# Second blocks of tokens of a pair's two heads share a step of differential attention; the second layer's memory logits two blocks at a time

## The chip, the cores and the metric

The kernel runs on one core of a Trainium2 chip. A core has a matrix engine (TensorE, PE in the profile, with its weight loads as PEld), a vector engine (VectorE, DVE), a scalar engine (ScalarE, ACT), a general engine (GpSimd, POOL) and an engine that issues most transfers (SyncE, SP). Each runs its own list of instructions in order and waits on semaphores for the others. The metric is device time in microseconds (us) for one execution, the median of several runs; lower is better.

## The reference, cut to what matters

Two layers on 512 tokens of width 1024. Layer 0 mixes tokens by differential attention: 6 heads, each with two query/key maps of width 64 and values of width 128. Tokens are handled in 4 blocks of 128 rows; block i of a head sees keys up to its own chunk, so it needs 128(i+1) keys. Layer 1 mixes by gated linear attention (4 heads). In both layers a cross attention of 4 heads into 256 memory tokens runs beside it, and both results go through one output projection; a gated MLP follows.

```python
logits = jnp.einsum('bhmqd,bhmkd->bhmqk', qb, k)         # m: the two maps of a head
logits = jnp.where(visible, logits + bias, -jnp.inf)
p = jax.nn.softmax(logits, axis=-1)
w = p[:, :, 0] - lam * p[:, :, 1]
o = jnp.einsum('bhqk,bhkv->bhqv', w, v)
...
o = rms_norm(o, out_norm_g) * (1.0 - lam_init)
# beside it, in both layers:
p = jax.nn.softmax(jnp.einsum('bqhd,bkhd->bhqk', q, k), axis=-1)   # k, v: 256 memory tokens
cross = jnp.einsum('bhqk,bkhd->bqhd', p, v)
x = x + jnp.concatenate([mix, cross], axis=-1) @ w_out[i]
```

## The kernel before

**Order.** The order of TensorE's instructions is the program's own, written out by hand. ACT, DVE, POOL and SP get their order from a scheduler at compile time, which takes what is ready by its reckoning, earlier written instructions first; once compiled, each of these lists is fixed too.

**Filler.** The large products are cut into units and put into a queue `F` (class `Filler`). `gemm` makes units of 6 matmuls of 512 columns, 1.296 us of credit each; `out_proj` units of 3 matmuls, 0.65 us. `F.fill(us)` adds credit and emits units until it is used up; `F.need(name)` emits until a marked point; `F.flush()` emits all. Every product is three matmuls (high and low parts of the split operands; ACT makes the high part of a weight block at L203, DVE the low part at L206).

**The loop of layer 0** (`diff_layer`) has 18 steps, three for a head: blocks 2 and 0 together (512 columns), block 1 alone (256 columns), block 3 alone (512). A turn t of the loop writes, for TensorE: `logits(t)` (L648, both maps, into the two PSUM banks with tag `lg`), `values(t-2)` (L686, into a bank `sm` that a head keeps until its last block), every third turn `finish` of an earlier head, filler, `turn(t-1)` (transposes of the finished weights, bank `tp`, copied out by ACT at L674), the memory attention's part, and filler again. There are two banks of each tag (`lg`, `sm`, `tp`, `mm`), used in rotation: whoever takes a bank waits until its last reader is done.

Beside TensorE a step goes: DVE adds the bias and takes the maximum (L653), ACT takes the exponential (L656), DVE inverts sums and joins the two maps (L661, L662, L664). When a head's last block has its values, ACT squares (L692), both normalise, and DVE writes `o` (L696). `finish(h)` transposes `o` into a bank `tp`, and ACT (L260) and DVE (L261) read the bank into the split tiles `mix[h]` that the output projection takes.

`prepare(h)` transposes queries and keys of a head into two `tp` banks, ACT copies both (`qT`, `kT`, L615); `logits` of that head need both. `norms(pair)` normalises queries and keys of a pair on ACT and DVE (L333, L334, L337). `keys1` makes the second layer's memory keys in a bank `lg` (ACT at L506). `MemAttn.logits(b)` writes one block of tokens into the two banks `lg` (L537); DVE and ACT do its softmax (L540, L544, L548); `MemAttn.turn(u)` transposes half a block (bank `tp`, copied at L557 by DVE or ACT); `MemAttn.values(pair)` takes a bank `sm` (L571) and splits it by L260 and L261, twice in turn.

**Layer 1** (`gla_layer`): four gate products (L858) into banks `lg` and `sm` in turn, read by DVE at L863 and L865, then the memory attention in a loop of 6 turns with `F.fill(4.0)` each, then the heads, `gate(1)`, `F.fill(8.0)` and `finish(1)`, which transposes three tiles with `F.fill(1.2)` after each, and a flush. Its transposes need `rr`, written by DVE at L980.

Of the kernel before, what the change touches and what calls it, by code (L numbers as in the profile page):

```python
# [11 lines left out]
F32 = mybir.dt.float32  # L12
# [9 lines left out]
S = 512  # L22
# [11 lines left out]
STEPS, FILL = (11, 18), (3.7, 1.64, 1.5)  # L34

TOGETHER = ((2, 0), (1,), (3,))
# [95 lines left out]
def trunk(ctx, tc, head_d, x_t, mem_t, wpack, cols_a_d, cols_d, conv_d, gate_d, rel_bias, diff_lambda, consts, onehot, out):  # L132
# [381 lines left out]
    class MemAttn:  # L514
# [16 lines left out]
        def logits(self, b):  # L531
            sm, rc = small("smm")[:, :4], small("rcm")[:, :4]
            pl = bank("lg"), bank("lg")
            for hp in range(2):
                for j in range(2):
                    hh = blk(j, 64)
                    mm(pl[j][:, blk(hp, 256)], self.qT[hp][hh, blk(b)], kmT[self.l][hh, hp], start=True, stop=True)  # L537
# [23 lines left out]
        def values(self, pair):  # L561
# [3 lines left out]
            po = bank("sm")  # L565
# [12 lines left out]
    def diff_layer(pool, mix, acc):  # L578
# [22 lines left out]
        heads = {}  # L601
# [5 lines left out]
        def prepare(h):  # L607
            pr, j = divmod(h, 2)
            t2 = []
            for src, g, nm in zip(qk[pr], (c_dq, c_dk), ("qT", "kT")):  # L610
                dst = pool.tile([128, S], F32, name=nm, bufs=3)
                p = bank("tp")
                for b in range(NB):
# [3 lines left out]
            sm = cp.tile([128, 16], F32, name="smd", tag="smd")  # L617
            heads[h] = dict(q=t2[0], k=t2[1], s2=sm.rearrange("p (m b) -> p m b", b=8),
                            nm=small("nmd"), rc=small("rcd"), v=vs[pr], j=j)
# [4 lines left out]
        def members(t):  # L624
            h, s = divmod(t, 3)
            out, at = [], 0
            for i in TOGETHER[s]:
                out.append((i, slice(at, at + 128 * (i + 1)), at))
                at += 128 * (i + 1)
            return h, out, at  # L630

        def logits(t):
            h, group, _ = members(t)
            H = heads[h]
            s2, nm, rc = H["s2"], H["nm"], H["rc"]
            if t % 3 == 0:
                bt = H["bt"] = pool.tile([128, S], F32, name="bt", bufs=2)
                src = bass.AP(tensor=bias_d.tensor, offset=bias_d[h].offset + 1, ap=[[1, 128], [1, 512]])
                nc.sync.dma_start(bt, src)
                G.memset(bt[0:64, 0:64], -1e30)  # L640
            pls = bank("lg"), bank("lg")
            for i, _, at in group:
                nk = 128 * (i + 1)
                cuts = (0, nk) if i == 0 else (0, nk // 2, nk)
                for k0, k1 in zip(cuts, cuts[1:]):
                    for m in range(2):
                        hh = blk(m, 64)
                        mm(pls[m][:, at + k0:at + k1], H["q"][hh, blk(i)], H["k"][hh, k0:k1], start=True, stop=True)  # L648
            e = xtile(), xtile()
            for m in range(2):  # L650
                for i, c, _ in group:
                    n1 = nm[:, 2 * i + m:2 * i + m + 1]
                    V.tensor_tensor_reduce(  # L653
                        out=e[m][:, c], in0=pls[m][:, c], in1=H["bt"][:, 127 + 128 * i::-1], scale=-1.0,
                        scalar=1e38, op0=ALU.add, op1=ALU.min, accum_out=n1)
                    A.activation(e[m][:, c], e[m][:, c], AF.Exp, scale=-1.0, bias=n1,  # L656
                                 accum_out=s2[:, m, i:i + 1])
            ids = sorted(i for i, _, _ in group)
            b = slice(ids[0], ids[-1] + 1, 2)
            lr = rc[:, 4 + ids[0]:4 + ids[-1] + 1:2]  # L660
            V.reciprocal(rc[:, b], s2[:, 1, b])  # L661
            V.scalar_tensor_tensor(lr, rc[:, b], nlam, s2[:, 0, b], op0=ALU.mult, op1=ALU.mult)  # L662
            for i, c, _ in group:
                V.scalar_tensor_tensor(e[1][:, c], e[1][:, c], rc[:, 4 + i:5 + i], e[0][:, c],  # L664
                                       op0=ALU.mult, op1=ALU.add)
# [11 lines left out]
        def values(t):  # L677
            h, group, _ = members(t)
            H = heads[h]
            if t % 3 == 0:  # L680
                F.need(f"v{h // 2}")
                H["po"] = bank("sm")
            po, wT = H["po"], live.pop(t)
            for i, _, at in group:
                for kb in range(i + 1):
                    mm(po[:, blk(i)], wT[:, at + 128 * kb:at + 128 * kb + 128], H["v"][:, kb, blk(H["j"])],  # L686
                       start=kb == 0, stop=kb == i)
            if t % 3 == 2:
                rs, ss, sq = small("rs0")[:, :NB], small("ss")[:, :NB], xtile()
# [537 lines left out]
```

## Time and profile before

| | |
|---|---|
| median of 3 runs | 1180.74 us (1180.72 to 1180.92) |
| the profiled execution | 1180.98 us |
| its span (first to last instruction) | 1179.2 us |
| what lies around the span | 1.78 us |
| TensorE busy | 1168.3 us of the span |
| VectorE, ScalarE busy | 757.1 us, 547.1 us |
| granted TensorE clock, mean | 0.999 |

Layer 0's loop stands at about 44 to 232 us of the span, layer 1's memory attention at 641 to 676 us, its `finish(1)` at 793 to 798 us. A matmul's shown duration overlaps the next one's, so the pace of TensorE is read from start to start, and its idle time from the view of waits. A row of the waits reads: engine, bank and line that waited, what ended the wait, total us, times, longest us.

### The profile page before, as it was taken

What the parts mean: (1) busy time and instruction counts of PE and PEld (TensorE: products, weight loads), DVE (VectorE), ACT (ScalarE), POOL (GpSimd) and SP (SyncE); (2) the same over time, 40 slices, a digit from 0 to 9 for tenths busy, and PEclk for the clock granted to TensorE, in tenths of its full rate; (3) what the DMA queues carried; (4) which work ended last, traced back from release to release, by engine and by line L of the source; (5) the groups of instructions that cost most, each with busy time, mean ns of one, the idle gap of its engine ahead of it and who ended that gap; (6) DMA issues with size and microseconds to landing.
All of it is one profiled execution on the core that took longest, in us unless ns stands there. A gap on an engine that the chain in (4) does not pass through costs nothing.

```text
span 1179.2 us, 14803 instructions
## 1 busy us (share of the span) xinstructions
PE 1168.3 (99%) x5658; PEld 966.6 (82%) x5658; DVE 757.1 (64%) x1252; ACT 547.1 (46%) x952; POOL 4.6 (0%) x25
## 2 busy tenths in 40 slices
PE   9999999999999999999999999999999999999998
PEld 7887877888888888888887888987888888888887
DVE  7567677597767335777557656768776743476741
ACT  6676576565444213344437534536443422343420
POOL 0000000000000000000000000000000000000000
PEclk9999999999999999999999999999999999999999
DMA  8432214132323232223341221243232233232231
GB/s 287 140 94 95 76 51 138 59 125 99 116 72 108 89 108 92 104 73 108 126 144 56 72 72 58 76 151 109 72 122 92 81 116 107 72 125 73 80 108 44
DMA packets 39556, 117.68 MB, mean 100 GB/s; under 512 B 4703, under 2 KB 7192, under 8 KB 39486
## 3 DMA queue, kind: packets, MB, share of 16 engines
q1 hardware_dynamic: 39054, 116.35, 29.3%
q8 instruction: 44, 0.72, 0.3%
q10 hardware_dynamic: 432, 0.39, 0.1%
q14 instruction: 26, 0.21, 0.1%
HBM read 112.52 MB, written 4.21 MB: 99 GB/s over the span
## 4 chain that ended last, share of the span: by engine, by line
PE 95%; ACT 2%; DVE 2%; issue 1%; POOL 0%; DVEq 0%; ACTq 0%; POOLq 0%
PE ps_mm L299 9%; PE ps_mm L298 9%; PE ps_mm L300 9%; PE ps_sm L300 7%; PE ps_sm L299 7%; PE ps_sm L298 7%; PE ps_mm L279 5%; PE ps_mm L281 5%; PE ps_mm L280 5%; PE ps_lg L298 3%; PE ps_lg L299 3%; PE ps_lg L300 3%; PE ps_tp L298 3%; PE ps_tp L299 3%; PE ps_tp L300 3%; PE ps_tp L172 2%
## 5 line engine op out<-in xcount | busy, mean ns | idle before, releaser
L203 ACT CAST whi<-raw 128x1024 fp32r<-128x1024 f32 (+4 forms) x212 | 207.7, 985 | 244.5 <-PE ps_tp L299 120.9
L206 DVE TENSOR_TENSOR wlo<-raw,whi 128x1024 fp32r<-128x1024 f32 (+4 forms) x212 | 240.6, 1140 | 94.0 <-ACT whi L203 91.4
L298 PE MATMUL ps_mm<-xsh,whi 128*128 128x512 f32 x438 | 173.0, 395 | 0.0
L299 PE MATMUL ps_mm<-xsl,whi 128*128 128x512 f32 x438 | 170.6, 390 | 0.8 <-DVE xsl L261 0.8
L300 PE MATMUL ps_mm<-xsh,wlo 128*128 128x512 f32 x438 | 170.6, 390 | 0.0
L298 PE MATMUL ps_sm<-xsh,whi 128*128 128x512 f32 x378 | 147.1, 389 | 0.0
L300 PE MATMUL ps_sm<-xsh,wlo 128*128 128x512 f32 x378 | 147.1, 389 | 0.0
L299 PE MATMUL ps_sm<-xsl,whi 128*128 128x512 f32 x378 | 147.0, 389 | 0.0
L279 PE MATMUL ps_mm<-whi,xsh 128*128 128x512 f32 (+2 forms) x352 | 136.1, 387 | 0.1
L281 PE MATMUL ps_mm<-whi,xsl 128*128 128x512 f32 (+2 forms) x352 | 131.0, 372 | 0.4 <-DVE xsl L261 0.4
L280 PE MATMUL ps_mm<-wlo,xsh 128*128 128x512 f32 (+2 forms) x352 | 130.6, 371 | 0.0
L1084 ACT ACTIVATE cvo<-u,cv 128x512 f32<-128x512 f32 x88 | 71.6, 815 | 123.1 <-DVE u L1082 123.1
L299 PEld LDWEIGHTS ps_mm<-xsl,whi 128*128 128x128 f32 x438 | 82.3, 188 | 18.1 <-DVE xsl L261 1.1
L298 PEld LDWEIGHTS ps_mm<-xsh,whi 128*128 128x128 f32 x438 | 82.3, 188 | 17.3 <-issue 0.5
L300 PEld LDWEIGHTS ps_mm<-xsh,wlo 128*128 128x128 f32 x438 | 82.2, 188 | 17.2
L1085 DVE SCALAR_TENSOR_TENSOR cvo<-u,cv,cvo 128x512 f32<-128x512 f32 x88 | 65.9, 750 | 39.8 <-ACT cvo L1084 39.7
L300 PEld LDWEIGHTS ps_sm<-xsh,wlo 128*128 128x128 f32 x378 | 71.0, 188 | 14.7
L298 PEld LDWEIGHTS ps_sm<-xsh,whi 128*128 128x128 f32 x378 | 71.0, 188 | 14.7
L299 PEld LDWEIGHTS ps_sm<-xsl,whi 128*128 128x128 f32 x378 | 71.0, 188 | 14.7
L279 PEld LDWEIGHTS ps_mm<-whi,xsh 128*128 128x128 f32 x352 | 66.2, 188 | 13.6 <-issue 3.3
L281 PEld LDWEIGHTS ps_mm<-whi,xsl 128*128 128x128 f32 x352 | 66.1, 188 | 12.4 <-DVE xsl L261 0.6
L280 PEld LDWEIGHTS ps_mm<-wlo,xsh 128*128 128x128 f32 x352 | 66.4, 189 | 9.9
(273 smaller groups left out, 1745.6 us busy)
## 6 DMA issues: line engine op xcount, KB each, us to landing
raw<-in_wpack_dram SPq DMA_DIRECT2D x178, 512.0 KB, 3.5
xt<-in_x_t_dram SPq DMA_DIRECT2D x15, 256.0 KB, 4.8
raw<-in_wpack_dram SPq DMA_DIRECT2D x15, 256.0 KB, 3.0
raw<-in_wpack_dram SPq DMA_DIRECT2D x8, 384.0 KB, 3.9
xres<-xt SPq DMA_DIRECT2D x8, 256.0 KB, 2.3
xt<-xres SPq DMA_DIRECT2D x8, 256.0 KB, 4.2
out_dram<-xt SPq DMA_DIRECT2D x7, 256.0 KB, 2.0
bt<-bias_d SPq DMA_DIRECT2D x6, 256.0 KB, 4.6
```

Source lines behind the costliest of these rows:

```text
L172: nc.tensor.transpose(dst, src, ident[:n, :n])
L203: ins = A.copy(hi[:, c], raw[:, c])
L206: V.tensor_sub(lo[:, c], raw[:, c], hi[:, c].bitcast(F32))
L279: mm(p, sh[k][:, blk(b)], hi, start=k == 0, stop=False)
L280: mm(p, sh[k][:, blk(b)], lo, start=False, stop=False)
L281: mm(p, sl[k][:, blk(b)], hi, start=False, stop=k == KT - 1)
L298: mm(p, hi[:, blk(n)], bh, start=i == first, stop=False)
L299: mm(p, hi[:, blk(n)], bl, start=False, stop=False)
L300: mm(p, lo[:, blk(n)], bh, start=False, stop=i == last)
L1084: A.activation(c, u[:, 2:], AF.Identity, scale=cv[l][:, 2, j:j + 1], bias=cv[l][:, 3, j:j + 1])
L1085: V.scalar_tensor_tensor(c, u[:, 1:S + 1], cv[l][:, 1, j:j + 1], c, op0=ALU.mult, op1=ALU.add)
```

## The change

Layer 0's attention is grouped by pairs of heads, 5 steps of 512 columns for a pair: blocks 2 and 0 of the first head, its block 3, block 1 of both heads, blocks 2 and 0 of the second head, its block 3. So 15 steps take the place of 18, in a loop of 18 turns in place of 21. The matmuls of each block stay as they are.

With it go: new filler credits (`STEPS`, `FILL`), the second share of a turn cut in two halves, with `prepare` between them (before: at the turn's end); `prepare` of a pair's first head one turn ahead of its first logits, and in the turns after a `prepare` the logits stand behind `values`; `norms`, `finish`, `load_x`, `out_proj`, `keys1` in other turns; layer 0's memory values in a bank `lg` in place of `sm`, and its memory logits in turns 5, 6, 7 and 9. In layer 1 the memory logits take two blocks at a time, the second block in the two banks `sm`; the loop's filler is (5.0, 4.0, 3.5, 5.0, 4.0, 2.5) in place of 6 times 4.0, and the fill ahead of `finish(1)` is 5.6 in place of 8.0.

```diff
-STEPS, FILL = (11, 18), (3.7, 1.64, 1.5)
-TOGETHER = ((2, 0), (1,), (3,))
+STEPS, FILL = (8, 11), (4.75, 2.1, 1.55)
+TOGETHER = (((0, 2), (0, 0)), ((0, 3),), ((0, 1), (1, 1)), ((1, 2), (1, 0)), ((1, 3),))
+NT = 3 * len(TOGETHER)
+PREPARE, FINISH = {4: 2, 5: 3, 9: 4, 10: 5}, {6: 0, 8: 1, 11: 2, 13: 3, 16: 4}
+MLOGITS, MVALUES = {5: 0, 6: 1, 7: 2, 9: 3}, {8: 0, 11: 1}
...
-        def logits(self, b):
+        def logits(self, *blocks):
+            banks = [(bank(tag), bank(tag)) for _, tag in zip(blocks, ("lg", "sm"))]
+            for b, pl in zip(blocks, banks):
+                for hp in range(2):
+                    for j in range(2):
+                        hh = blk(j, 64)
+                        mm(pl[j][:, blk(hp, 256)], self.qT[hp][hh, blk(b)], kmT[self.l][hh, hp], start=True, stop=True)
+            for b, pl in zip(blocks, banks):
+                self.softmax(b, pl)
...
-        def values(self, pair):
+        def values(self, pair, tag="sm"):
...
-            po = bank("sm")
+            po = bank(tag)
...
-        for t in range(21):
+        for t in range(NT + 3):
...
-            if t == 10:
+            if t == 8:
                 ops1, keys1 = mem_kv(1)
                 ops1()
+            if t == 14:
+                keys1()
+            if t == 10:
+                load_x(x_t)
+            if t == 11:
+                out_proj(0, mix, 0, None)
             if t == 16:
-                keys1()
-            if t == 12:
-                load_x(x_t)
-                out_proj(0, mix, 0, None)
-            if t == 18:
                 rest = out_proj(0, mix, 1, acc, 5)
             f = FILL[bisect(STEPS, t)]
-            m = t - M0
-            if t < 18:
+            new = t - 1 in PREPARE
+            if t < NT and not new:
                 logits(t)
-            if 0 <= t - 2 < 18:
+            if 0 <= t - 2 < NT:
                 values(t - 2)
-            if t % 3 == 0 and t >= 6:
-                finish(t // 3 - 2)
-            if t == 6:
+            if t < NT and new:
+                logits(t)
+            if t in FINISH:
+                finish(FINISH[t])
+            if t == 5:
                 keys0("tp")
             F.fill(f)
-            if t in (4, 10):
-                norms((t + 2) // 6, 0)
-                norms((t + 2) // 6, 1)
-            if 0 <= t - 1 < 18:
+            if t in (3, 8):
+                norms((t + 2) // 5, 0)
+                norms((t + 2) // 5, 1)
+            if 0 <= t - 1 < NT:
                 turn(t - 1)
-            if 1 <= m < 5:
-                ma.turn(2 * m - 2)
-            if m in (3, 5):
-                ma.values(m // 2 - 1)
-            if 0 <= m < 4:
-                ma.logits(m)
-            if t == 20:
+            if t - 1 in MLOGITS:
+                ma.turn(2 * MLOGITS[t - 1])
+            if t in MVALUES:
+                ma.values(MVALUES[t], "lg")
+            if t in MLOGITS:
+                ma.logits(MLOGITS[t])
+            if t == NT + 2:
                 F.flush()
-            F.fill(f)
-            if 1 <= m < 5:
-                ma.turn(2 * m - 1)
+            F.fill(f / 2)
+            if t in PREPARE:
+                prepare(PREPARE[t])
+            F.fill(f / 2)
+            if t - 1 in MLOGITS:
+                ma.turn(2 * MLOGITS[t - 1] + 1)
             if t == 3:
                 ma.queries()
-            if t in (5, 6, 11, 12):
-                prepare(2 * ((t + 1) // 6) + (t + 1) % 6)
-            if t == 20:
+            if t == NT + 2:
                 finish(5)
...
-        for t in range(6):
-            if 0 < t < 5:
-                ma.turn(2 * t - 2)
-                ma.turn(2 * t - 1)
-            if t in (3, 5):
-                ma.values(t // 2 - 1)
-            if t < 4:
-                ma.logits(t)
-            F.fill(4.0)
+        for t, f in enumerate((5.0, 4.0, 3.5, 5.0, 4.0, 2.5)):
+            if t % 3:
+                for j in range(2):
+                    ma.turn(4 * (t // 3) + 2 * (t % 3 - 1) + j)
+            else:
+                if t == 3:
+                    ma.values(0)
+                ma.logits(*((0, 1), (2, 3))[t // 3])
+            F.fill(f)
+        ma.values(1)
...
-        F.fill(8.0)
+        F.fill(5.6)
         finish(1)
```

`members`, `logits`, `values` and `prepare` follow the new grouping: sums, maxima and inverses stand in tiles of a pair, the bias of a head is loaded at its first logits (a new function `bias`), and the normalisation of a head's output is a function `output`, called when its fourth block has its values.

107 lines of the change are left out of this document (55 added, 52 removed).

## The prediction

> **What bounds the kernel now.** I read the page first (busy time, the chain that ended last), then the waits of TensorE, then the stretches around layer 0's loop, then single instructions in order of time.
>
> ```profile
> span 1179.2 us, 14803 instructions
> PE 1168.3 (99%) x5658; PEld 966.6 (82%) x5658; DVE 757.1 (64%) x1252; ACT 547.1 (46%) x952; POOL 4.6 (0%) x25
> PE 95%; ACT 2%; DVE 2%; issue 1%; POOL 0%; DVEq 0%; ACTq 0%; POOLq 0%
> ```
>
> TensorE is the bound: it idles 1179.2 - 1168.3 = 10.9 us in all, and the change neither adds nor drops a matmul. It can only change TensorE's waits and the small losses where it passes from one kind of work to another. The waits by who ended them:
>
> ```profile
> PE ps_lg L648 <- ACT kT L615: 2.1, 2, 1.2
> PE ps_mm L299 <- DVE xsl L261: 0.8, 1, 0.8
> PE ps_tp L172 <- DVE xsl L261: 0.7, 1, 0.7
> PE ps_tp L172 <- ACT xt L674: 0.7, 1, 0.7
> PE ps_tp L172 <- DVE xt L548: 0.7, 2, 0.4
> PE ps_lg L648 <- ACT kmT L506: 0.4, 1, 0.4
> ```
>
> Six rows, 5.4 us, all in places that the change rewrites. In layer 0 most fall where ACT and DVE are full:
>
> ```profile
> 160.00:170.00 10.00, 10.00 (x59) 8.50 (x58) 6.99 (x18) 9.85 (x29) 0.00 (x0) 1.00 0.00 1
> 170.00:180.00 10.00, 9.33 (x69) 7.30 (x69) 9.97 (x28) 7.55 (x19) 0.00 (x0) 1.00 0.53 172
> ```
>
> (us, then busy time of PE, PEld, DVE, ACT, POOL, then the granted clock.) Here the third pair's norms meet softmax and weight splits: ACT 9.85 of 10, then DVE 9.97.
>
> **Waits that go.** (a) The 2.1 us behind `kT` are two logits written straight behind their own `prepare`. After, half a fill and `values` stand between: 2.8 + 0.9 us at the second pair, 1.4 + 0.9 us at the third, against waits of at most 1.2. Gone: -2.1. (b) The 0.7 behind `xsl` (L261) is the third use of a `tp` bank in a row after `finish(1)`; after, 5.6 us of filler follow that finish. -0.7. (c) The 0.7 behind L674 is taken up below. (d) Layer 1's two waits behind L548 are turns 4 us behind their logits; after, 5.0 of fill and a second block's logits lie between. -0.7. (e) The 0.8 at L299 is the output projection reaching a tile that `finish(1)` has just transposed, with too little filler left.
>
> ```profile
> 788.07 0.95 DVE L980 TENSOR_TENSOR rr<-rr,go 128x768 f32<-128x768 f32 x1
> 792.61 0.60 PE L172 MATMUL ps_tp<-C,rr 128*128 128x128 f32 x4
> ```
>
> 2.4 us less ahead of the transposes puts them at 792.6 - 2.8 (4 units of 0.7) = 789.8, still behind `rr` at 789.0, and leaves those 2.8 us for the tiles: -0.8. If DVE brings `rr` 0.8 us later, this comes back. (f) The wait behind L506 stays: `keys1` still stands right ahead of logits.
>
> **Fewer, fuller pieces.** What an interruption of the filler costs, from one run of 18 matmuls:
>
> ```profile
> 155.64 0.40 PE L280 MATMUL ps_mm<-wlo,xsh 128*128 128x512 f32 x1
> 159.28 0.40 PE L281 MATMUL ps_mm<-whi,xsl 128*128 128x512 f32 x1
> 159.52 0.60 PE L172 MATMUL ps_tp<-C,xt 128*128 128x128 f32 x4
> ```
>
> The run began at 155.30. From its second to its last start are 16 steps: 3.64 / 16 = 0.2275 us each. 159.52 - 155.30 = 4.22 is 0.12 over 18 x 0.2275. Walking the credits through both loops gives 588 filler matmuls in either, in 41 runs before and 36 after: 5 x 0.12 = -0.6. The pieces themselves, from the chain in order of time (values of 512 and of 256 columns):
>
> ```profile
> 64.17 1.09 PE ps_sm L686 x8
> 73.44 0.64 PE ps_sm L686 x4
> ```
>
> Two values of 256 columns cost 1.28, one of 512 costs 1.09: -0.19 for a pair; logits lose one start, which I put between nothing and the same 0.2. Three pairs: between -0.6 and -1.1 with both; some of it is the same loss as in the runs, so -1.2 for all together. What DVE and ACT save (three copies, three pairs of tiny operations) is off TensorE's path: nothing.
>
> **New waits.** (g) The heaviest that I can place. At turn 11 the queue is empty, the output projection's units are added, and the order is `values(9)`, `logits(11)`, `finish(2)`, fill. The third unit takes `mix[2]`, which that finish has only just transposed; before, it came a turn later. A finish behind a softmax step waits for the step's exponentials on ACT:
>
> ```profile
> 107.17 0.60 PE L172 MATMUL ps_tp<-C,o 128*128 128x128 f32 x4
> 110.79 0.75 DVE L261 SCALAR_TENSOR_TENSOR xsl<-ps_tp,cols,xsh 128x512 fp32r<-128x512 f32 x1
> 205.07 0.60 PE L172 MATMUL ps_tp<-C,o 128*128 128x128 f32 x4
> 207.31 0.67 ACT L260 ACTIVATE xsh<-ps_tp,cols 128x512 fp32r<-128x512 f32 x1
> 208.01 0.75 DVE L261 SCALAR_TENSOR_TENSOR xsl<-ps_tp,cols,xsh 128x512 fp32r<-128x512 f32 x1
> ```
>
> From first transpose to the end of L261: 4.4 us at 107, 3.7 at 205. The unit's second matmul wants it about 0.4 + 7 x 0.23 = 2.0 us behind that start (four transposes, six matmuls of the units ahead, its own first). Wait 1.7 to 2.4; with engines free at once (0.6 + 0.67 + 0.75) nothing. Taken: +1.7, the later row being the nearer stage. Behind it are queued all of TensorE's later pieces.
>
> (h) At turn 10 the filler runs out inside the turn: `prepare(5)` is followed at once by a memory turn that needs its first `tp` bank.
>
> ```profile
> 191.00 0.60 PE L172 MATMUL ps_tp<-C,qs 128*128 128x128 f32 x4
> 191.97 0.71 PE L648 MATMUL ps_lg<-kT,qT 64*128 64x128 f32 x8
> 192.24 0.69 ACT L615 ACTIVATE qT<-ps_tp,cols 128x512 f32<-128x512 f32 x1
> ```
>
> In this row, as after, the copy of the last memory products goes first on ACT. The next transposes could start 0.97 behind the first, `qT` is read at 1.93: +0.95; with ACT free, 0.97 to 0.6 + 0.69 = 1.3, so +0.3.
>
> (i) Memory values in a bank `lg` make the next logits wait for the split. The same in layer 1 with `sm`:
>
> ```profile
> 640.89 1.13 PE L537 MATMUL ps_lg<-kmT,xt 64*128 64x256 f32 x8
> 641.77 0.69 DVE L863 SCALAR_TENSOR_TENSOR xt<-ps_sm,xt 96x512 f32<-96x512 f32 x1
> 662.30 1.97 PE L571 MATMUL ps_sm<-xt,vm 128*64 128x128 f32 x32
> 664.20 1.14 PE L537 MATMUL ps_lg<-kmT,xt 64*128 64x256 f32 x8
> 665.61 0.42 DVE L261 SCALAR_TENSOR_TENSOR xsl<-ps_sm,xsh 128x256 fp32r<-128x256 f32 x1 [0.45 <-ACT xsh L260]
> ```
>
> The split ends 666.03 - 664.20 = 1.83 us behind the values. In layer 1, the first block's logits cover 1.1 (1.13 at L537, with some overlap) and the second's first matmul 0.2 more: +0.5; and in its first turn that second bank is free only at 641.77 + 0.69 = 642.46, where it is wanted at about 640.89 + 1.3 = 642.2: +0.2. One run more in its loop: +0.1. In layer 0 turn 12 covers 1.4 and a little: +0.3 (up to 1.0 behind other work). At turn 8 the cover is 3.2 us, enough if the split runs at once. But it stands behind the norms:
>
> ```profile
> 168.53 1.04 PE L172 MATMUL ps_tp<-C,xt 128*128 128x128 f32 x8
> 173.75 0.56 ACT L674 COPY xt<-ps_tp 128x512 f32<-128x512 f32 x1
> 175.53 0.68 DVE L557 COPY xt<-ps_tp 128x512 f32<-128x512 f32 x1
> 179.15 1.23 DVE L337 TENSOR_TENSOR ks<-ks,rs_y 128x1024 f32<-128x1024 f32 x1
> ```
>
> Two turns written right behind the norms at 168.5 were copied out 5.8 and 7.7 us later; that is wait (c), and its likeness after has about as much cover (a memory turn, values of 1.9 and two fills of 1.4; before, a memory turn and 18 matmuls, 4.2): +0.7, with the split slipped in between as before's softmax was; 0.3 if the copies come earlier; the high end is a rival below. (j) `finish(4)` stands behind head 5's squares:
>
> ```profile
> 226.27 1.05 PE L686 MATMUL ps_sm<-v,xt 128*128 128x128 f32 x8
> 227.36 0.37 ACT L692 ACTIVATE xt<-ps_sm,rs 128x128 f32<-128x128 f32 x1 [1.70 <-PE ps_sm L686]
> 228.40 0.37 ACT L692 ACTIVATE xt<-ps_sm,rs 128x128 f32<-128x128 f32 x1
> ```
>
> Squares end 1.7 us behind the values; with 0.67 + 0.75 that is 3.1, wanted at 0.44 + 10 x 0.23 = 2.8: +0.3 (0 to 0.7). (k) The third pair's first logits need `kT` behind one memory softmax on ACT, 2.3 us of cover for 1.3 to 1.5: +0.2 (0 to 1.2).
>
> **Transfers.** The same loads in the same order on SP; x is loaded two turns earlier, one turn ahead of its use in place of the same turn. The bias of each head finds its slot free one step or more ahead. Nothing; the waits of SP are not TensorE's today.
>
> **Sum.** Gone: 2.1 + 0.7 + 0.7 (c) + 0.7 + 0.8 + 1.2 = 6.2. New: 1.7 + 0.95 + 0.8 + 0.3 + 0.7 + 0.3 + 0.2 = 4.95. Net -1.25. The profiled execution took 1180.98 (1179.2 and 1.78 around it); the runs' median is 0.24 lower. 1180.98 - 1.25 - 0.24 = **1179.5 us**, 0.1% under 1180.74: no change that can be told, if 0.2% (2.4 us) is what a measurement of this kernel can tell.
>
> **Rivals.** *The new waits do not come* (faster): the scheduler puts the finish's copies ahead of the exponentials, ACT is free for `qT`, splits run at once. Low ends: 0 + 0.3 + 0.4 + 0 + 0.3 + 0 + 0 = 1.0 for 4.95, so 1175.5. For it: at 205 L260 waited 1.6 us behind the transposes' end for nothing but its turn on ACT. Against: it waited so at 107 too, and the scheduler's rule has not changed. Half-way, 1177.5.
>
> *The bank `lg` behind the norms decides* (slower): at turn 8 the memory values' split queues behind the norms' whole backlog, whose last operation ended 180.4 - 168.5 = 11.9 us behind their place; `logits(9)` wants the bank 5.9 us behind it. A wait of 6 + 1, less the 0.7 counted: +6.3, 1185.8. It decides from a wait of 4.4 us on (1179.5 - 0.7 + 4.4 is 2.4 over before). For it: DVE 9.97 of 10. Against: the copies at 173.75 and 175.53 were written behind the norms and ran ahead of their last operation, so the backlog lets later work through; a split that ends 1.8 us behind the second copy (7.7) gives a wait of 3.6, 1182.4.
>
> *The regrouping does nothing for the time*: waits return one for one in the same burst, since DVE and ACT have no less to do there, and only the runs are saved. 1180.74 - 1.2 = 1179.5: the same number, from another cause; it counts with the forecast.
>
> *The clock falls*. At the kernel's start matmuls take nearly twice their later time:
>
> ```profile
> 6.42 0.85 PE ps_mm L463 x2
> 8.68 1.36 PE ps_mm L463 x6
> ```
>
> 0.43 against 0.227 each. Were a wait long enough to bring that back for about 3 us, it would cost 1.5 us more, on top of the slow rival: 1187. In this profile waits up to 1.2 us left the clock at 1.00. The Trainium skill, page "TensorE: Matmul & The Clock Gate", section "HAM oscillation — how this bites in real kernels", gives the point: idle gaps over about 3.4 us send the clock to half. By that rule none of the waits of my sum does it, and the slow rival's does; no run here shows it yet.
>
> **Numbers.** Forecast (waits traded, 1178.4 to 1182): 0.46. New waits mostly absent: 0.31. Slow rival: 0.19. Clock: 0.04. Of the forecast's 0.46, 0.02 lie below and 0.01 above the 0.2%: faster 0.31 + 0.02 = 0.33, within 0.43, slower 0.19 + 0.04 + 0.01 = 0.24. Range: 1176.0, near the low ends, to 1184.3, short of the slow rival's full price.
>
> **What would show it.** Right: no wait behind `kT`, a wait of 1.5 to 2.5 us at L281 of the output projection's third unit behind L261 just after `finish(2)`, about 1 us at a transpose behind L615 near turn 10, 0.5 us at L537 in layer 1 behind L261, L299 gone. Wrong: a wait behind L615 that stays; new waits of TensorE under 2 us or over 8 us in all; a clock under 1.00; or filler pieces that cost other than 0.12.

## The result and the profile after

| | before | after |
|---|---|---|
| median (9 runs each) | 1180.92 us (1180.12 to 1182.29) | 1184.55 us (1182.23 to 1185.54) |
| ratio of after to before | | 1.0025, 95% interval 1.0014 to 1.0035 |
| the profiled execution | 1180.98 us | 1184.87 us |
| layer 0: first logits to last `finish` | 187.92 us | 193.27 us |

The changed kernel is slower, by 0.14 to 0.35%. The forecast of 1179.5 us was wrong, and so was its range, which ended at 1184.3. The page of the changed kernel: span and busy time, and the shares of the chain that ended last.

```profile
span 1183.1 us, 14792 instructions
PE 1170.4 (99%) x5658; PEld 969.0 (82%) x5658; DVE 754.4 (64%) x1246; ACT 547.4 (46%) x949; POOL 4.6 (0%) x25
PE 94%; DVE 3%; ACT 2%; issue 1%; DMA 0%; POOL 0%; DVEq 0%; ACTq 0%; POOLq 0%
```

The same 5658 matmuls; TensorE's idle time went from 10.9 to 12.7 us, and its busy time, which should not have moved, from 1168.3 to 1170.4. That second number is the first hint that matmuls themselves took longer somewhere. Where the 3.9 us of the span arose is read from four rows of the order in time, the first logits and the last `finish` of layer 0. Before:

```profile
44.05 0.43 PE L648 MATMUL ps_lg<-kT,qT 64*128 64x192 f32 x2
231.97 0.49 PE L172 MATMUL ps_tp<-C,o 128*128 128x128 f32 x3
```

and after (line numbers are those of the changed kernel: L648 is now L662, L686 L703, L674 L691, L615 L625, L261 L266, L281 L286, L299 L304):

```profile
44.06 0.43 PE L662 MATMUL ps_lg<-kT,qT 64*128 64x192 f32 x2
237.33 0.49 PE L177 MATMUL ps_tp<-C,o 128*128 128x128 f32 x3
...
168.03 0.69 PE L662 MATMUL ps_lg<-kT,qT 64*128 64x256 f32 x2
170.45 1.76 PE L662 MATMUL ps_lg<-kT,qT 64*128 64x256 f32 x6 [1.72 <-DVE rs_y L186]
172.14 2.08 PE L703 MATMUL ps_sm<-v,xt 128*128 128x128 f32 x8
173.87 0.61 PE L284 MATMUL ps_mm<-whi,xsh 128*128 128x512 f32 x1
```

Layer 0 lost 193.27 - 187.92 = 5.35 us; the rest of the kernel gained 1.5. The last four rows are turn 9: its first two logits matmuls run, then TensorE idles 1.72 us, and then six logits matmuls and eight of the values take 173.87 - 170.45 = 3.42 us, about twice what they need in the kernel e1 below. The waits of TensorE, all kinds over 0.3 us:

```profile
PE ps_lg L662 <- DVE rs_y L186: 1.7, 1, 1.7
...
PE ps_mm L304 <- DVE xsl L266: 1.1, 2, 0.9
PE ps_lg L662 <- ACT kT L625: 1.1, 1, 1.1
PE ps_tp L177 <- ACT qT L625: 1.0, 1, 1.0
PE ps_tp L177 <- ACT xt L691: 0.7, 1, 0.7
PE ps_tp L177 <- DVE xsl L266: 0.6, 1, 0.6
PE ps_sm L542 <- DVE xsl L266: 0.4, 1, 0.4
PE ps_mm L303 <- ACT xsh L265: 0.4, 1, 0.4
```

(Two rows are left out: a wait at the kernel's start, and 0.4 at L286, which the kernel before has at L281.) The largest new one names `rs_y` at L186, an operation of the norms that has nothing to do with a bank `lg`. VectorE's own list shows what was meant; it is the changed kernel's, in order of time:

```profile
168.33 0.42 DVE L266 SCALAR_TENSOR_TENSOR mxl<-ps_lg,mxh 128x256 fp32r<-128x256 f32 x1
168.67 1.22 DVE L342 TENSOR_TENSOR qs<-qs,rs_y 128x1024 f32<-128x1024 f32 x1
...
169.88 0.42 DVE L266 SCALAR_TENSOR_TENSOR mxl<-ps_lg,mxh 128x256 fp32r<-128x256 f32 x1
170.22 0.17 DVE L186 SCALAR_TENSOR_TENSOR rs_y<-rs_t,rs_y 128x16 f32<-128x16 f32 x1
```

The memory values of turn 8 ended at 164.6. The second half of their split (L266) ran at 169.88 to 170.30, between the norms' operations, and the logits went on at 170.45: that split was what held the bank, and L186 is merely the next row. TensorE's clock over the stretch, in windows that end where it changes:

```profile
167.32:170.73 3.41, 1.69 (x10) 1.05 (x10) 3.38 (x13) 1.49 (x4) 0.00 (x0) 1.00 0.46 159
170.73:174.14 3.41, 3.41 (x15) 2.67 (x13) 2.22 (x5) 0.74 (x3) 0.00 (x0) 0.50 0.02 7
174.14:177.55 3.41, 3.41 (x19) 2.67 (x19) 1.39 (x5) 2.95 (x14) 0.14 (x1) 1.00 0.80 235
```

(From the left: the window, its length, busy time of PE, PEld, DVE, ACT, POOL, the granted clock, then the share and rate of the DMA engines.) In the 3.41 us behind the wait the granted clock was 0.50, which costs half of 3.41, 1.7 us. It does not fall in every execution: three of the nine runs had a mean clock of 1.000 and took 1182.23 to 1182.96 us; the six at 0.997 to 0.999 took 1184.28 to 1185.54.

### The profile page after: what moved, and what is told of

Its sections match the earlier page's. It is cut to its first block, busy times and chain, and to the rows that moved or that the text cites. A ratio compares the mean times of both kernels' runs of the same rounds, so it can differ in the third digit from the quotient of the medians.

```text
span 1183.1 us, 14792 instructions
## 1 busy us (share of the span) xinstructions
PE 1170.4 (99%) x5658; PEld 969.0 (82%) x5658; DVE 754.4 (64%) x1246; ACT 547.4 (46%) x949; POOL 4.6 (0%) x25
## 4 chain that ended last, share of the span: by engine, by line
PE 94%; DVE 3%; ACT 2%; issue 1%; DMA 0%; POOL 0%; DVEq 0%; ACTq 0%; POOLq 0%
PE ps_mm L304 9%; PE ps_mm L305 8%; PE ps_mm L303 8%; PE ps_sm L305 7%; PE ps_sm L303 7%; PE ps_sm L304 7%; PE ps_mm L284 6%; PE ps_mm L286 5%; PE ps_mm L285 5%; PE ps_lg L304 3%; PE ps_lg L305 3%; PE ps_lg L303 3%; PE ps_tp L304 3%; PE ps_tp L303 3%; PE ps_tp L305 3%; PE ps_tp L177 2%
## 5 line engine op out<-in xcount | busy, mean ns | idle before, releaser
L304 PE MATMUL ps_mm<-xsl,whi 128*128 128x512 f32 x438 | 170.8, 390 | 1.1 <-DVE xsl L266 1.1
L304 PE MATMUL ps_sm<-xsl,whi 128*128 128x512 f32 x378 | 147.1, 389 | 0.0
L286 PE MATMUL ps_mm<-whi,xsl 128*128 128x512 f32 (+2 forms) x352 | 131.1, 372 | 0.4 <-DVE xsl L266 0.4
L304 PEld LDWEIGHTS ps_mm<-xsl,whi 128*128 128x128 f32 x438 | 82.3, 188 | 18.8 <-DVE xsl L266 1.8
L304 PEld LDWEIGHTS ps_sm<-xsl,whi 128*128 128x128 f32 x378 | 71.0, 188 | 14.8
L286 PEld LDWEIGHTS ps_mm<-whi,xsl 128*128 128x128 f32 x352 | 66.2, 188 | 12.4 <-DVE xsl L266 0.6
```

The lines of the kernel that those rows point to most:

```text
L286: mm(p, sl[k][:, blk(b)], hi, start=False, stop=k == KT - 1)
L304: mm(p, hi[:, blk(n)], bl, start=False, stop=False)
```

## The experiments

The theory after reading: layer 0 lost 2.1 us (start to start) to the bank `lg` behind the norms, 1.7 to the clock that this wait brought down, and the rest to smaller waits at turns 9 to 11. The rivals: the waits only move, since VectorE and ScalarE are full; the clock fell for another reason. Layer 0 below is the stretch from first logits to last `finish` of one profiled execution. Ratios are to the kernel before, on the same chip. In e2, e3 and e8 the stretch holds one fall of the clock (1.7 us), as in the changed kernel, but some 20 us later.

| run | median us | ratio (95%) | layer 0, us |
|---|---|---|---|
| changed kernel | 1184.55 | 1.0025 (1.0014 to 1.0035) | 193.27 |
| e7_layer1_only | 1179.25 | 0.9984 (0.9975 to 0.9993) | 187.91 |
| e8_layer0_only | 1187.11 | 1.0052 (1.0038 to 1.0066) | 193.14 |
| e1_norms_late | 1180.75 | 0.9999 (0.9990 to 1.0007) | 189.55 |
| e2_pe_busy_in_wait | 1183.43 | 1.0018 (1.0009 to 1.0027) | 193.01 |
| e3_oproj_order | 1185.37 | 1.0036 (1.0023 to 1.0050) | 192.74 |
| e5_prepare_first | 1180.78 | 1.0002 (0.9993 to 1.0011) | 189.66 |
| e6_oproj_early | 1180.24 | 0.9997 (0.9989 to 1.0006) | 189.11 |
| e56_both | 1180.59 | 1.0000 (0.9991 to 1.0008) | 189.23 |
| e13_split_after_softmax | 1179.89 | 0.9993 (0.9984 to 1.0002) | 188.82 |
| e10_early_and_order | 1179.72 | 0.9991 (0.9982 to 0.9999) | 188.33 |
| e11_all_four | 1179.57 | 0.9991 (0.9982 to 1.0000) | 188.58 |
| e14_values_on_sm | 1178.33 | 0.9980 (0.9971 to 0.9989) | 187.21 |

### Which part costs

e7 is the kernel before with layer 1's edits alone, e8 the changed kernel with layer 1 as before:

```diff
 e7: kernel before +
-        for t in range(6): ... ma.logits(t) ... F.fill(4.0)
+        for t, f in enumerate((5.0, 4.0, 3.5, 5.0, 4.0, 2.5)): ... ma.logits(*((0, 1), (2, 3))[t // 3])
-        F.fill(8.0)
+        F.fill(5.6)
 e8: the changed kernel with these lines turned round
```

> The kernel of before with the second layer's part of the change alone (memory logits two blocks at a time, the new list of fills, 5.6 for 8.0); the differential attention keeps its 18 steps. Theory A (the two parts are independent, layer 1 gains what the stage marks showed, 1.5 us): 1179.2 to 1179.7, ratio 0.9988. Rival B (the mark's difference is a shift of fill between the layers, no gain by itself): 1180.6 to 1181.2. Rival C (my prediction's own sum for layer 1, a gain of 0.7): 1180.0 to 1180.4.

> The changed kernel with the second layer as before (memory logits block by block, 8.0 for 5.6): the differential attention's 15 steps alone. Theory A (the parts are independent): 1.5 to 2 us over the changed kernel, 1186 to 1186.5, about 1.0045 of the kernel before. Rival B (the second layer's gain was only a shift of filler): 1184.5.

Layer 1's part alone is worth 1.6 thousandths, about 1.9 us; layer 0's part alone costs 5.2 thousandths, about 6.1 us. They add up to +4.2 us, and the changed kernel shows +3.0 us (0.0025) with an interval of 1.2 either way; e8 is 0.6 over its range. By the stretches the parts are independent (187.91 and 193.14 against 187.92 and 193.27): two edits of opposite sign under one result, theory A in both.

### The bank behind the norms

```diff
             if t in (3, 8):
-                norms((t + 2) // 5, 0)
-                norms((t + 2) // 5, 1)
+                (turn 3: both norms; turn 8: only F.need("qk2"))
             ...
             if t in MVALUES:
                 ma.values(MVALUES[t], "lg")
+            if t == 8:
+                norms(2, 0)
+                norms(2, 1)
```

> The norms of the third pair are written behind the memory values of turn 8 instead of ahead of them, so that the two split instructions that empty the memory values' lg bank no longer stand behind them on VectorE and ScalarE; TensorE's order is the same. Theory A (the lg bank behind the norms is the new wait, and the clock falls because of it): the idle time of L662 behind L186 (1.7 us) goes to under 0.3, the granted clock stays at 1.00 in 166 to 176 us, and the time is 3 to 4 us under the changed kernel's profiled 1184.9, i.e. 1181 to 1182. Rival B (the wait only moves: prepare(4) in turn 9 is then late by the norms' length): 1 to 2 us come back as waits of L177 behind the group norm, 1182.5 to 1184. Rival C (the excess of layer 0 isn't here): 1184 to 1185.

1180.75, just under theory A's range, and a ratio of 0.9999 for 1.0025: an edit that leaves TensorE's list as it is brings the kernel level with the one before. Four waits of e1 in layer 0 (those of 0.6 behind `xsl` and 0.4 behind `xsh` are as in the changed kernel, the others under 0.3), its clock, and TensorE at the place of the wait:

```profile
PE ps_tp L177 <- ACT xt L691: 1.4, 1, 1.4
PE ps_lg L662 <- ACT kT L625: 1.2, 1, 1.2
PE ps_mm L304 <- DVE xsl L266: 1.1, 2, 0.9
PE ps_tp L177 <- ACT qT L625: 0.5, 1, 0.5
```

```profile
168.00:170.00 2.00, 2.00 (x16) 1.57 (x13) 1.88 (x7) 1.32 (x4) 0.00 (x0) 1.00 0.19 76
170.00:172.00 2.00, 2.00 (x10) 1.68 (x9) 1.97 (x8) 2.00 (x11) 0.00 (x0) 1.00 0.00 0
```

```profile
167.47 1.13 PE L662 MATMUL ps_lg<-kT,qT 64*128 64x256 f32 x8
168.54 1.16 PE L703 MATMUL ps_sm<-v,xt 128*128 128x128 f32 x8
169.45 0.48 PE L284 MATMUL ps_mm<-whi,xsh 128*128 128x512 f32 x1
```

The row with `rs_y` is gone and TensorE is busy throughout at full clock; logits and values of turn 9 take 169.45 - 167.47 = 1.98 us. Layer 0 is 3.7 us shorter, what wait (2.1) and clock (1.7) came to. `prepare(4)` does not wait for the norms, so rival B is out. The other waits stayed (the two at `prepare(5)` make 1.9 us in place of 1.7); they are taken up below.

Next, the wait kept and TensorE made busy in it:

```diff
             pls = bank("lg"), bank("lg")
+            if t == 9:
+                for n in range(8):
+                    mm(pls[0], mix[0][0][:, :128], mix[0][0], start=True, stop=True)
```

> Eight extra 512-column matmuls (some 1.8 us of TensorE, their result is overwritten at once and not used) go into the first lg bank of the logits of turn 9, ahead of the real ones: TensorE is busy for about the length of the wait, and the real logits still begin when the second bank comes free. Theory A (the wait makes the granted clock fall for 3.4 us): no row of clock under 1.00 in 166 to 176 us, and the time falls by 1.5 to 2 us although TensorE does more work: about 1183, with all runs close together. Rival B (the clock falls for another reason, such as the whole stretch's load): the clock still falls, and the time stays at 1184 to 1186. Rival C (the matmuls themselves come too late or delay the logits): the wait stays and 0.5 to 1.8 us are added to 1184.5.

The median came to 1183.43; its interval overlaps that of the changed kernel, so the time settles nothing. The profile does, in three stretches of e2:

```profile
166.00:170.00 4.00, 4.00 (x21) 2.90 (x21) 3.97 (x15) 1.83 (x6) 0.00 (x0) 1.00 0.53 201
186.16:189.58 3.42, 1.76 (x11) 1.06 (x10) 3.31 (x7) 3.03 (x7) 0.00 (x0) 1.00 0.83 312
189.58:192.99 3.41, 3.41 (x17) 3.19 (x17) 0.02 (x1) 1.60 (x4) 0.00 (x0) 0.50 0.69 198
```

The clock did not fall behind turn 9, although the logits still came late. It fell 20 us further on instead, behind a stretch in which two waits at `prepare(5)` left TensorE 1.66 us idle in 3.42. So there was no fall in 166 to 176 us, as theory A had it, but the runs were not all close together: a second place was as near to the edge as the first. Nor is the missing fall a proof of theory A. e8, and e3 below, keep the wait of turn 9 (1.7 and 1.8 us), and in their profiled executions the clock did not fall behind it either. In e3 the wait lay across the border of two of the windows in which the clock is set (see the last part of this section):

```profile
166.41:169.82 3.41, 2.03 (x11) 1.25 (x9) 3.41 (x13) 1.96 (x7) 0.00 (x0) 1.00 0.74 250
169.82:173.24 3.42, 3.02 (x19) 2.52 (x20) 2.83 (x8) 1.24 (x5) 0.00 (x0) 1.00 0.00 0
```

TensorE idled 1.38 us in the one and 0.40 in the other. In both kernels the clock fell behind `prepare(5)` instead, at 190.31 and 189.35, each time behind a window with 1.66 us idle. What brings the clock down is therefore decided by e15 to e18, not by e2.

### The smaller waits

In e3 the units of the output projection that need `mix[2]` come third for each pair of tiles:

```diff
         if late is None:
+            if l == 0:
+                units.sort(key=lambda u: (u[0] // 2, u[1] == len(kk[u[0] // 2]) - 1, u[0]))
             return give(units)
```

> The units of the first output projection are handed out so that those that need mix[2] come third for each pair of output tiles (first both units of tiles 0 and 1 that need mix[0] and mix[1], then the two that need mix[2]); two mm banks stay open for that. Theory A (the third unit waits for finish(2)'s split, 1.7 us, TensorE idle): that wait goes, waits of L304 behind xsl fall from 1.1 us to under 0.4, and the time is 1.2 to 1.7 us under the changed kernel's: about 1183. Rival B (the fill between is only consumed earlier, and the time comes back where fill is then missing): no change, 1184.5.

A miss: 1185.37. The wait at L304 went from 1.1 to 0.2 us, but this row of TensorE's list is new:

```profile
202.16 1.13 PE L662 MATMUL ps_lg<-kT,qT 64*128 64x128 f32 x14 [0.79 <-DVE mxl L266]
```

TensorE now reaches the logits of turn 12 earlier, and stands before the other bank `lg` that memory values have taken, those of turn 11. Rival B.

e5, on top of e1, writes `prepare(4)` ahead of the memory logits in turn 9:

```diff
-            if t in MLOGITS:
+            if t in MLOGITS and t != 9:
                 ma.logits(MLOGITS[t])
             ...
             if t in PREPARE:
                 prepare(PREPARE[t])
+            if t == 9:
+                ma.logits(3)
```

> As e1_norms_late, and in turn 9 the transposes of prepare(4) are issued ahead of the memory logits of block 3 instead of behind them, so that on ScalarE the copy into kT stands ahead of the four memory exponentials. Theory A (kT is late only because of those exponentials): the wait of L662 behind kT (1.2 us in e1) goes to under 0.2 and the time is 1.0 to 1.3 us under e1's 1180.75: about 1179.6. Rival B (the queue behind is what counts: the third pair's stretch is bound by VectorE and ScalarE, and the wait moves to prepare(5)): the waits of L177 behind ps_tp grow by as much, 1180.3 to 1180.9.

No gain: 1180.78. The wait behind `kT` went, and the first row of e5's waits grew from 1.4, 1 to 2.2, 2:

```profile
PE ps_tp L177 <- ACT xt L691: 2.2, 2, 1.3
```

The transposes of `prepare(4)` now came before ScalarE had copied turn 8's bank.

e6, on e1, has e3's order and hands the output projection's units out in turn 10; e56 has e5 as well.

```diff
             if t == 10:
                 load_x(x_t)
-            if t == 11:
                 out_proj(0, mix, 0, None)
```

> As e1_norms_late, with e3's order of units and the first output projection's units handed out one turn earlier (turn 10), so that units that need only mix[0] and mix[1] can run around prepare(5), where the filler had run out. Theory A (TensorE lacks filler there): the two waits at prepare(5) (1.4 and 0.5 us) shrink to under 0.7 together, the third unit's wait is gone, time 1178 to 1179.5, and the granted clock is 1.00 in every window of every run. Rival B (VectorE and ScalarE bound the stretch from turn 8 to turn 12, so TensorE only waits elsewhere, as in e3 where 1.1 us taken away gave 0.8 back at L662 behind mxl): 1180.5 to 1181.5.

> e5 and e6 together: prepare(4) first, the output projection's units one turn earlier and in the new order. Theory A (independent waits): the sum of both gains, 1177 to 1178.5, under both kernels. Rival B (VectorE and ScalarE bound turns 8 to 12): not better than the better of the two by more than 0.3 us.

e6's 1180.24 lies between its two ranges; its waits are rival B's, with 0.9 us new at turn 12's logits as in e3. e56's 1180.59 is rival B too. The filler of turn 10 was used up by the memory products before it came to the new units, so the two waits at `prepare(5)` are unchanged in e6. What makes turn 9's copy late had to be looked for. VectorE in e1, in order of time:

```profile
179.13 0.96 DVE L211 TENSOR_TENSOR wlo<-raw,whi 128x768 fp32r<-128x768 f32 x1 [0.41 <-ACT whi L208]
182.07 0.96 DVE L211 TENSOR_TENSOR wlo<-raw,whi 128x768 fp32r<-128x768 f32 x1 [1.98 <-DMA raw<-in_wpack_dram]
182.94 0.55 DVE L669 CUSTOM_DVE_ANT_0 xt<-ps_lg,bt 128x384 f32<-128x384 f32 x1
```

The logits of turn 10 ended at 179.5. Their first reduction (L669) ran at 182.94, behind a weight split that is written later in the program, that the scheduler had put first, and that stood waiting 1.98 us. Everything that follows on ScalarE, the exponentials and the copy of turn 9 (L691), was late by that. It might also be why e5 and e6 did next to nothing, so they are repeated with the order kept. e13 (on e1), e10 (on e6), e11 (on e56) pin the four reductions and exponentials of turn 10 and that turn's weight copies in written order:

```diff
+                    if t == 10:                      (the reductions and the exponentials)
+                        tc.keep_in_program_order(ins)
...
-        if pin:
+        if pin or hot[0]:                            (the weight copies of turn 10)
             tc.keep_in_program_order(ins)
```

> As e1_norms_late, and in turn 10 the weight splits (L208 and L211) keep their written place behind the reductions and exponentials of that turn's logits; in e1 two of the splits stood ahead of them on VectorE, the second waiting 1.98 us for its transfer, so that the reductions began 3.4 us after the logits had ended. Theory A (this queueing makes turn 9's copy late, and that is the wait of 1.4 us at prepare(5)): the wait of L177 behind L691 shrinks to under 0.5, its follower (0.5 us) goes, time 1.0 to 1.9 us under e1, about 1179.3. Rival B (the wait only moves on, to finish(2) and its third unit): 1180.3 to 1181.

> e6_oproj_early with the weight splits of turn 10 behind that turn's softmax. Theory A: the waits at prepare(5) (1.4 and 0.5 us in e6) go to under 0.6 together, no window of 3.41 us holds more than 1.3 us of idle TensorE, so no run's clock falls; 1178.2 to 1179.2. Rival B (VectorE and ScalarE are full there, the wait moves to the logits of turns 11 and 12): 1180.0.

> e10 and e5's order in turn 9 (prepare(4) ahead of the memory logits). Theory A: 0.2 to 1.2 us under e10, since kT's wait (1.2) goes and turn 8's copy is still 0.8 late. Rival B: as e10 or above it, because the memory exponentials move behind and their turn is late.

e13's reduction ran 0.9 us behind the first split's start:

```profile
179.27 0.96 DVE L211 TENSOR_TENSOR wlo<-raw,whi 128x768 fp32r<-128x768 f32 x1 [0.41 <-ACT whi L208]
180.15 0.55 DVE L669 CUSTOM_DVE_ANT_0 xt<-ps_lg,bt 128x384 f32<-128x384 f32 x1
```

The wait behind L691 (1.4 us) went, 1.0 us behind `qT` stayed in place of 0.5, and layer 0 is 0.7 us shorter than in e1: about half of what theory A had asked. e10, at 1179.72, missed its range too (up to 1179.2), and e11, at 1179.57, is rival B. The order is worth 0.65 to 0.8 us in layer 0 wherever it is kept (e1 to e13, e6 to e10, e56 to e11). e6's edit gives the same 0.4 to 0.5 us with it as without, and e5's still nothing that can be told, so the late reductions are not why these two did little.

e14 is e11 with the memory values of turn 11 in a bank `sm`:

```diff
             if t in MVALUES:
-                ma.values(MVALUES[t], "lg")
+                ma.values(MVALUES[t], "lg" if t == 8 else "sm")
```

> e11 with the second memory values (turn 11) in a bank of tag sm instead of lg, so that the logits of turn 12 don't wait for the split behind it (0.9 us at L662 behind mxl in e6). Theory A: that wait goes, 0.7 to 1.1 us under e11. Rival B (the split is late for the sm bank's next user, the values of turn 13, as well, or the exponentials are): within 0.3 of e11.

1178.33 against 1179.57 for e11 on the same chip: 1.2 us, a little more than theory A. The waits of e14 in layer 0 over 0.3 us:

```profile
PE ps_tp L177 <- ACT xt L695: 1.0, 2, 0.8
PE ps_tp L177 <- ACT qT L625: 1.0, 1, 1.0
PE ps_tp L177 <- DVE xsl L266: 0.6, 1, 0.6
```

No wait for a bank `lg` of memory values is left. e14 is faster than both kernels, by 0.1 to 0.3% over the one before. Of that, layer 1 alone gives 0.16% (e7), and the two intervals overlap; by the profiles' stretches, 15 steps with all these edits are 187.21 against 187.92 for 18 steps, 0.7 us. The regrouping itself is worth little, and as written it cost 5.35 in the profiled execution.

### What brings the clock down

In the profiles so far the clock fell behind windows of 3.41 us with 1.66 to 1.72 us idle, at distances from the first record of the clock that are whole multiples of 3.413 us (in the changed kernel 163.84 = 48 x 3.413, in e2 184.32 = 54 x 3.413). Four kernels put ten waits of one length into the first layer's feed-forward of e14, where TensorE is busy otherwise. Their extra matmuls are not used for anything.

```diff
                     ug = up(wg, n)
+                    if l == 0 and q and n:
+                        p = bank("tp")
+                        mm(p[:, 0:128], idl[:, 0:128], idl[:, 0:128], start=True, stop=True)
+                        for _ in range(2):      # e16: 3, e17: 4
+                            G.memset(idl, 0.0)
+                        (e18: mm(p, idl[:, 0:128], idl, start=True, stop=True) and two more clearings)
+                        mm(p[:, 128:256], idl[:, 0:128], idl[:, 0:128], start=True, stop=True)
```

> e14_values_on_sm with ten waits of TensorE put into the first layer's feed-forward, where it is busy otherwise: a matmul that reads a tile, two clearings of that tile by GpSimd (0.52 us each by the profile's rows of that shape), a matmul that reads it again; ten waits of some 1.2 to 1.4 us, about 21 us apart. Theory A (the clock falls to half for 3.41 us when TensorE idled for 1.66 us or more of a window of 3.41 us on a grid; in the profiles so far it fell behind windows with 1.66 to 1.72 and did not behind 1.38): no fall, time 1178.3 + 10 x (1.3 + 0.25) = about 1193 to 1195. Rival B (only a wait over 3.4 us lowers the clock): the same. Rival C (a fall comes from the crowded stretch of turns 8 to 12, not from waits as such): the same.

> The same with three clearings, ten waits of some 1.7 to 1.9 us. Theory A: of the ten, those fall whose window happens to hold 1.66 us or more of the wait, about half, each 3.41 us at half clock and 1.7 us of time: about five falls, 1178.3 + 10 x (1.8 + 0.25) + 5 x 1.7 = about 1207. Rivals B and C: no fall, about 1199.

> The same with four clearings, ten waits of some 2.2 to 2.4 us. Theory A: about seven of ten fall, 1178.3 + 10 x (2.3 + 0.25) + 7 x 1.7 = about 1216. Rivals B and C: no fall, about 1204.

> e15 with each wait of some 1.3 us followed by one matmul of 512 columns (about 0.9 us) and a second wait of 1.3 us, so that none is longer than in e15 but a window of 3.41 us holds up to 2.5 us of idle time. Theory A (the sum in the window counts): about six or seven of ten fall, 1178.3 + 10 x (2.6 + 1.15) + 6.5 x 1.7 = about 1227. Theory A' (the longest single wait counts): no fall, about 1216. Rivals B and C: no fall.

| run | waits | falls, profiled execution | mean clock of the runs | median us |
|---|---|---|---|---|
| e15 | ten of 1.28 | none | 1.000 | 1198.58 |
| e16 | ten of 1.87 | 2 | 0.996 to 0.997 | 1208.10 |
| e17 | ten of 2.45 | 7 | 0.990 to 0.993 | 1221.26 |
| e18 | ten pairs of 1.28 and 1.22 | 4, two of them of twice the length | 0.989 to 0.991 | 1233.61 |

(The lower clock at the kernel's end, which every profile shows from at most 1.3 us before the last instruction on, is not counted.) The times were 1 to 7 us over theory A's, mainly because one insertion cost 0.75 us beside its wait (e15) and not the 0.25 I had put; the falls decide. One window of e17 and the one behind it, and the same of e18:

```profile
322.39:325.80 3.41, 0.96 (x7) 0.73 (x6) 3.08 (x4) 1.69 (x2) 2.10 (x4) 1.00 0.54 161
325.80:329.21 3.41, 3.41 (x10) 2.63 (x9) 1.64 (x3) 1.25 (x2) 0.00 (x0) 0.50 0.38 147
```

```profile
374.18:377.60 3.42, 1.59 (x6) 0.53 (x4) 3.01 (x5) 1.78 (x2) 1.54 (x3) 1.00 0.57 155
377.60:381.01 3.41, 2.74 (x8) 2.26 (x9) 1.81 (x3) 1.25 (x2) 0.56 (x2) 0.50 0.56 157
```

Waits of 2.45 us lower the clock in a quiet stretch, so rivals B and C are out. In e18 no wait is longer than e15's, and e15's clock never fell: the sum in the window counts, and A' is out, though only four of ten fell where theory A had six or seven. Over all the profiles no window of the grid with less than 1.66 us idle was followed by a fall and every one with 1.9 or more was. In between both occur, and e16 shows both with the same idle time:

```profile
482.00:485.40 3.40, 1.53 (x10) 1.19 (x9) 3.08 (x4) 1.76 (x2) 1.57 (x3) 1.00 0.56 167
485.40:488.80 3.40, 3.40 (x10) 2.62 (x9) 1.99 (x4) 1.25 (x2) 0.00 (x0) 0.50 0.64 183
393.20:396.60 3.40, 1.54 (x9) 1.28 (x9) 3.16 (x4) 1.46 (x2) 1.57 (x3) 1.00 0.62 169
396.60:400.00 3.40, 3.40 (x16) 2.81 (x15) 1.41 (x3) 1.26 (x2) 0.00 (x0) 1.00 0.40 145
```

So the point is near half a window and the rows do not fix it; what else enters the count is open. e16's two falls are fewer than the five expected for that reason.

## Why the prediction was wrong

Two steps failed, and both lie at turn 8 and the turn behind it; a third group and the gain by fewer pieces were mis-sized.

**The clock.** "Were a wait long enough to bring that back": I had the fall as a rival at 0.04, on top of the slow rival alone, since waits up to 1.2 us had left the clock at 1.00 and I took the step to lie above 3 us. It lies near 1.7 us of idle time in 3.41, summed, and a wait of 1.72 reached it. That is 1.7 us of the 3.9 in the profiled execution. What the profile of before showed was read rightly, but 1.2 us excluded nothing between 1.2 and 3. The clock is not the whole error: the three runs at 1.000 lie inside the range, and still 1.3 to 2.0 us over the kernel before, where 1.25 under it had been forecast.

**Turn 8, the bank `lg`.** Taken at +0.7, "with the split slipped in between as before's softmax was"; measured 2.1 start to start. The split did slip in, but it is two pairs of operations, and the second pair waited for ScalarE's turn and for a 1.22 us multiplication of the norms. The slow rival named the mechanism, and its prices (3.6 and 6.3) and its point of decision (4.4) were too high. A wait of 2.1 with the clock's 1.7 and the misses below was enough. e1 shows the wait and the clock together: removed, they give back 3.7 us of layer 0.

**The burst around the third pair.** (h) was +0.95 for `prepare(5)` by the wait behind `qT`; measured 0.71 and 0.96 idle, at two transposes, about 2.0 start to start. I had not seen that turn 9's copy would stand behind weight splits that the scheduler draws forward. e13 showed that for e1, where VectorE's reductions came late. In the changed kernel's trace the reductions began at 184.49, 0.5 us behind their logits, and it was ScalarE's part of the splits that ran first: one of 0.84 us at 185.68, which had waited 2.10 us, ahead of the exponentials, and one of 1.03 us at 188.40 ahead of the copy at 189.34. No run moved these in the changed kernel itself. (k), +0.2 with an upper end of 1.2, measured 1.07: the end was right, the choice within it wrong. (b), -0.7, did not come: TensorE still waited 0.6 us for a bank behind `finish(1)`, at 162.13, because that split ended 7.1 us behind the first transpose of its finish (155.01 to 162.08).

**What held.** (g) +1.7 at the third unit was 0.40 and 0.88 idle, 1.7 start to start, and e3 confirmed its cause by removing it. (j) +0.3 was 0.2 idle, and turn 12's logits +0.3 were as foreseen. In layer 1, (d) and (e) went as predicted, and what came for them is 0.4 at L542 and 0.2 in the first turn. The layer gained 1.5 and not the 0.7 of my terms, in part because a wait costs 0.15 to 0.3 us more from start to start than its idle time shows: the two of (d) were 0.98 and not 0.7, the one of (e) 1.1 and not 0.8. That is 0.6 of the 0.8; the rest is open.

Added up: clock 1.7, turn 8 +1.4, (h) +1.05, (k) +0.95, (b) +0.7, layer 1 -0.8 make 5.0 over the predicted -1.25, and the profiled execution is 5.1 over it. That the sum closes so well is partly luck, for it takes the other terms as forecast, and one of them came only in part.

**Fewer, fuller pieces.** The -1.2 was mis-sized. Between layer 0's first logits and last `finish`, TensorE is busy 184.05 us in the kernel before and 184.09 in e14, both at a clock of 1.00; the 0.7 us that e14 gains are idle time (3.87 and 3.12). Busy time holds the slow start behind each wait, and e14 has seven waits over 0.1 us for five. With every wait priced from start to start against the same passage without one (4.6 us before, 4.5 in e14), the rest of the stretch is 183.3 and 182.75: by this estimate the pieces saved 0.6 us, half of the term. The waits of (a) and (c), which cost 0.3 more than their idle time, make up for part of the difference.

**The rivals.** The rival of new waits that do not come is refuted by the waits. "Regrouping does nothing for the time" is nearly what e14 shows.

## What to carry to other kernels

A wait is priced with the other idle time around it: sum TensorE's idle time over 3.4 us, and if it comes near half of that, add 1.7 us for the clock. Where a bank's reader is written behind long work on a full engine, count when its last operation runs; writing the reader first cost nothing and gave all of it back. Removing one wait in a stretch where VectorE and ScalarE are full mostly moves it (e3, e5, e6), until the work that holds their queues is itself moved (e13) or the shared bank is (e14).

## What the runs showed of the hardware that I had not expected

The granted clock is set window by window. The windows are 3.413 us long and lie on a grid; its first record lay 4.1 to 7.5 us into the span, from profile to profile, so the same wait lowers the clock in one execution and not in another, by where it falls: the wait of turn 9 did in the profile of the changed kernel and did not in those of e3 and e8. Six of nine runs of the changed kernel show a mean clock under 1.000, and eight of eleven of e1 show 1.000. (A mean of 0.999 alone proves no fall, because the lower clock at the kernel's end counts in it: the profiles of the kernel before and of e10 have 0.999 without one.) In a fallen window the clock is 0.50, and it returned after one window in 15 of the 17 falls inside the profiled kernels, after two in the other two (both e18), where the fallen window itself held 0.7 us of idle time. The Trainium skill, page "TensorE: Matmul & The Clock Gate", section "Part 1: The HAM clock gate (the "warmup" mystery)", has a free-running window of 3413 ns and a clock of one half after at least one idle window: the window's length, its free phase and the half agree with these runs (3.413 us, 0.50), the idle window does not, since about half of one was enough.
